# The products with the first scan batch's states, four projection steps later, in a decoder trunk on one core

## The chip, the core and the metric

The kernel runs on one core of a Trainium2 chip. The metric is the device time of one execution in microseconds (us). Engines are called by the names that the profile gives them: PE (TensorE, matrix products; its weight loads are PEld), DVE (VectorE), ACT (ScalarE), POOL (GpSimd), SP (SyncE, which here issues DMAs).

## The reference, cut to what matters

The program is a two-layer decoder trunk over 512 positions of width 1024. The change lies in layer 0, where one input projection feeds two mixers side by side: HGRN2 (a gated linear recurrence) and S5 (a complex diagonal state space model). What matters here of the S5 mixer and of the projections:

```python
proj = einsum('bld,df->blf', x, ev_w_in)          # 512 x 1024 times 1024 x 2560
q_a, f_a, i_a, g_a, u_b = split_cols(proj, [512, 512, 512, 512, 512])
# S5: 32 groups of 16 channels, 64 complex states each
drive = einsum('blgn,gpn->blgp', ug, bbar)         # real and imaginary part
h     = associative_scan(h[t] = abar * h[t-1] + drive[t])
y     = einsum('blgp,gnp->blgn', h_re, c_re) - einsum('blgp,gnp->blgn', h_im, c_im)
y     = gelu(y + d_skip * u);  z = y @ w_glu;  y_b = z[:, :512] * sigmoid(z[:, 512:])
```

HGRN2 needs q, f and g of the projection: silu(q), a log, a cumulative sum and an exp of f, silu(g). After the mixers come the output projection, a layer norm and a mixture of 16 experts; layer 1 has attention in place of the mixers.

## The kernel before, in words

Every float32 product is done as three products of halves (`hilo`, L194 to L196: ACT writes a rounded high part with a CAST, L195, and DVE subtracts it to get the low part, L196; `mm3`, L198 to L202, adds high*high, high*low and low*high in one accumulator). A weight chunk of 128 x 1024 (twice 128 rows of the contraction) is split this way three chunks ahead of its use (`split_upto`). All of this lives in a pool of 13 units `u`: raw weights, split weights and other large tiles take a unit when one is free, and the writer of a new tile waits for the last reader of the old one.

The projections of q, f and g are the main sequence of this stage: each has four chunks, and for each chunk four *steps* of six products (two rows of the contraction times three), each into one of four accumulators `acc`. In the fourth chunk each step ends with ACT's evacuation of the accumulator: Silu for q (L502), Sigmoid for f (L503), Silu for g (L505). This makes 48 steps. Between them `weave` (L57) puts pieces of a side sequence, a Python generator: a number yielded by the side says how many steps of the main sequence pass before the next piece is issued. All engines work through their instructions in the order in which they are issued, so `weave` sets the order on each of them.

The side is `s5_batches` (L916): four batches q of four pairs of groups. Within a batch:

- the *head* (L924 to L948): transposes of the input matrices VT (L928) and of the inputs U (L934), copied out of PSUM by ACT (V, L930; ut, L936), products for the inner matrix MM (L943) and their copies (L948); POOL prepares the next batch's tables
- after `YB[0]` = 1 step: the drives (L961), rotated by DVE with six operations (L964 to L969)
- after `YB[1]` = 2 steps: two scans and two products (L971 to L975)
- after `YB[2]` = 2 steps: the states H[0] (L977) and H[1] (L980)
- after `YB[3]` = 5 steps: the *products with the states* (L985, L987): for each of four r one product of ut with MM and two with H[0] and H[1], then DVE adds the result to Y (L989); the next batch's head follows at once.

The four batches take 10 steps each. Behind the last comes `glu_prep` (L993): the Gelu of Y on ACT (L998), then for four column blocks the transposes (L1005), a cast (L195) and a subtraction (L196) each. When the main sequence is at its end, what is left of the side is issued without steps in between, and then the GLU's products begin, whose first block ends with a product that needs the low part of the last weight chunk.

A second piece rides along in the g projection: `hgrn_f` (L539) gives one piece per step from step 33 on: four DVE operations on F (L544), Ln on ACT (L548), four scans on DVE (L551), Exp on ACT (L555, L556) and eight DVE products (L560, L561).

Of the kernel before, what the change touches and what calls it, by code (L numbers as in the profile page):

```python
# [35 lines left out]
YB = 1, 2, 2, 5, 0  # L36
# [16 lines left out]
def blk(i, n=128):  # L53
    return slice(i * n, (i + 1) * n)
# [23 lines left out]
def run_all(gen):  # L78
    for _ in gen:
        pass  # L80
# [82 lines left out]
class Trunk:  # L163
# [752 lines left out]
    def s5_batches(self, U, tabs):  # L916
        nc, s5, I = self.nc, self.s5, self.I
        Vv = nc.vector
        big = lambda nm: s5.tile([128, 4, 128], F32, name=nm)
        Y = U.rearrange("c r j g n -> c r j (g n)")  # L920
        f2 = lambda a: a.rearrange("p r c -> p (r c)")
        for q in range(4):
            ps, EP = slice(4 * q, 4 * q + 4), self.EPs[q % 2]
            Vm = []  # L924
            for i in range(2):
                tp = self.tp()
                for r in range(4):
                    nc.tensor.transpose(tp[:, blk(r)], self.VT[i][:, r].rearrange("p j g n -> p (j g n)"), self.idf)  # L928
                v = big(f"V{i}")
                nc.scalar.copy(v, tp.rearrange("p (r f) -> p r f", r=4))  # L930
                Vm.append(v)
            tp = self.tp()
            for r in range(4):
                nc.tensor.transpose(tp[:, blk(r)], U[:, 4 * q + r].rearrange("c j g n -> c (j g n)"), self.idf)  # L934
            ut = big("ut")
            nc.scalar.copy(ut, tp.rearrange("p (r f) -> p r f", r=4))  # L936
            nc.gpsimd.tensor_mul(Y[:, ps], Y[:, ps],
                                 self.dp[:, ps].rearrange("c r g n -> c r (g n)").unsqueeze(2).to_broadcast([128, 4, 4, 32]))
            nc.gpsimd.tensor_copy(self.R4[:, :, 1:128], self.r4[:, ps].unsqueeze(2).to_broadcast([128, 4, 127]))
            tm = self.tp()  # L940
            for r in range(4):
                for i in range(2):
                    nc.tensor.matmul(tm[0:32, blk(r)], self.BB[i][:, 4 * q + r].rearrange("p g n -> p (g n)"),  # L943
                                     EP[i][:, r, 0:4].rearrange("p k g n -> p (k g n)"),
                                     start=i == 0, stop=i == 1)
            tmv = tm.rearrange("p (r k f) -> p r k f", r=4, k=4)
            for j in range(4):
                nc.scalar.copy(self.MM[blk(j, 32), :, j:4, :], tmv[0:32, :, 0:4 - j, :])  # L948
            if q < 3:
                self.s5_inputs(q + 1)  # L950
                self.s5_outputs(q + 1)

            run_all(tabs)
            Tc, Ts = self.Tc[:, ps], self.Ts[:, ps]
            yield YB[0]

            dps = []
            for i in range(2):
                d = self.sd()
                for r in range(4):  # L960
                    nc.tensor.matmul(d[:, blk(r)], Vm[i][:, r, :], ut[:, r, :], start=True, stop=True)  # L961
                dps.append(d.rearrange("p (r c) -> p r c", r=4))
            g1, g2, h1, h2 = big("g1"), big("g2"), big("h1"), big("h2")
            Vv.tensor_mul(g1, dps[0], Tc)  # L964
            Vv.tensor_mul(h1, dps[1], Ts)
            Vv.tensor_mul(g2, dps[1], Tc)
            Vv.tensor_mul(h2, dps[0], Ts)
            Vv.tensor_add(g1, g1, h1)
            Vv.tensor_sub(g2, g2, h2)  # L969
            yield YB[1]  # L970
            Vv.tensor_tensor_scan(f2(h1), f2(self.R4), f2(g1), 0.0, op0=MUL, op1=ADD)  # L971
            Vv.tensor_tensor_scan(f2(h2), f2(self.R4), f2(g2), 0.0, op0=MUL, op1=ADD)
            a, b = slice(0, 127), slice(1, 128)
            Vv.tensor_mul(g1[:, :, a], h1[:, :, a], Tc[:, :, a])
            Vv.tensor_mul(g2[:, :, a], h2[:, :, a], Ts[:, :, a])  # L975
            yield YB[2]
            Vv.tensor_sub(self.H[0][:, :, b], g1[:, :, a], g2[:, :, a])  # L977
            Vv.tensor_mul(g1[:, :, a], h1[:, :, a], Ts[:, :, a])
            Vv.tensor_mul(g2[:, :, a], h2[:, :, a], Tc[:, :, a])
            Vv.tensor_add(self.H[1][:, :, b], g1[:, :, a], g2[:, :, a])  # L980
            yield YB[3]
            yp = self.sd()
            for r in range(4):
                o = yp[:, blk(r)]
                nc.tensor.matmul(o, ut[:, r, :], self.MM[:, r].rearrange("p l f -> p (l f)"), start=True, stop=False)  # L985
                for i in range(2):
                    nc.tensor.matmul(o, self.H[i][:, r, :], EP[i][:, r, 1:5].rearrange("p k g n -> p (k g n)"),  # L987
                                     start=False, stop=i == 1)
            Vv.tensor_add(Y[:, ps], Y[:, ps], yp.rearrange("c (r l f) -> c r l f", r=4, l=4))  # L989
            yield YB[4] if q < 3 else 3  # L990
        self.Y = Y
# [968 lines left out]
```

## Time and profile before

| | us |
|---|---|
| median of 3 runs | 991.99 (991.78 to 992.62) |
| the profiled execution's own time | 995.26 |
| its span, first to last instruction | 993.6 |
| PE busy | 859.7 (87%) |
| DVE busy | 789.4 (79%) |
| ACT busy | 571.9 (58%) |
| POOL busy | 292.1 (29%) |
| TensorE's mean granted clock | 0.945 of full |

The stage of the change lies between about 65 and 186 us of the span. A time in a timeline is that from the span's start. Products on PE overlap, so that a duration is longer than the distance from one start to the next, and the distance is what a product costs. A bracket at a row's end tells how long the engine was idle before it and which instruction ended that.

### The profile page before, as it was taken

The numbers are of one execution on the slowest core, as the hardware profiler recorded it, in microseconds if no ns is written. First come the engines' busy times: TensorE is split into PE (matmuls) and PEld (weight loads), VectorE is DVE, ScalarE is ACT, GpSimd is POOL, SyncE is SP. The second block draws the span as 40 slices with busy tenths as digits, with TensorE's granted clock in tenths as the row PEclk, the third lists the DMA queues.
The fourth block names the chain that finished last, engine by engine and source line by source line (L and its number), as shares of the span: only waits on it lengthen the run. The fifth ranks groups of instructions, "written<-read, shape, count | busy, mean of one in ns | idle before, by whom it ended". The sixth has DMA issues, their size and how long they took to land. (4 is left out here: it accounts for less than half of the span.)

```text
span 993.6 us, 13230 instructions
## 1 busy us (share of the span) xinstructions
PE 859.7 (87%) x4428; PEld 714.5 (72%) x4428; DVE 789.4 (79%) x1547; ACT 571.9 (58%) x936; POOL 292.1 (29%) x333
## 2 busy tenths in 40 slices
PE   6996999998975899999883899989994789999964
PEld 5895887787873688878662787878883668888742
DVE  7998668667679799989577757889778879999657
ACT  3331445635114889988673446666612589999741
POOL 6397981100102132221230002355611232322210
PEclk9998999999996999999897999999997799999977
DMA  8321112101946799999875350230093869999842
GB/s 274 138 87 43 43 43 94 45 1 46 361 191 231 293 296 361 393 359 309 294 246 180 129 127 1 97 74 2 1 344 148 344 222 322 374 369 362 273 126 84
DMA packets 52731, 192.02 MB, mean 193 GB/s; under 512 B 13355, under 2 KB 15415, under 8 KB 38192
## 3 DMA queue, kind: packets, MB, share of 16 engines
q1 hardware_dynamic: 37344, 156.47, 43.1%
q0 software_dynamic: 13296, 24.14, 9.3%
q10 hardware_dynamic: 2016, 10.49, 2.6%
q8 instruction: 38, 0.62, 0.3%
q14 instruction: 37, 0.30, 0.1%
HBM read 183.20 MB, written 31.46 MB: 216 GB/s over the span
## 5 line engine op out<-in xcount | busy, mean ns | idle before, releaser
L200 PE MATMUL acc<-u 128*128 128x512 f32 (+1 forms) x712 | 297.3, 418 | 7.3 <-ACT u L195 7.3
L202 PE MATMUL acc<-u 128*128 128x512 f32 (+1 forms) x712 | 282.8, 397 | 5.8 <-DVE u L196 5.6
L201 PE MATMUL acc<-u 128*128 128x512 f32 (+1 forms) x712 | 282.4, 397 | 3.4 <-POOL u L196 1.9
L196 DVE TENSOR_TENSOR u<-u 128x1024 fp32r<-128x1024 f32 x142 | 172.4, 1242 | 27.5 <-ACT u L195 26.5
L196 DVE TENSOR_TENSOR u<-rx,u 128x1024 fp32r<-128x1024 f32 x128 | 152.4, 1221 | 31.5 <-ACT u L195 30.3
L195 ACT CAST u<-u 128x1024 fp32r<-128x1024 f32 x150 | 152.9, 1050 | 42.5 <-PE acc L202 36.7
L202 PEld LDWEIGHTS acc<-u 128*128 128x128 f32 x712 | 142.0, 199 | 37.2 <-DVE u L196 9.3
L200 PEld LDWEIGHTS acc<-u 128*128 128x128 f32 x712 | 143.8, 202 | 31.2 <-ACT u L195 9.9
L201 PEld LDWEIGHTS acc<-u 128*128 128x128 f32 x712 | 142.7, 200 | 25.9 <-DVE u L196 3.4
L195 ACT CAST u<-rx 128x1024 fp32r<-128x1024 f32 x128 | 129.4, 1048 | 5.4 <-issue 3.0
L1615 POOL DMA_INDIRECT yd<-row,r x36 | 57.0, 1583 | 228.8 <-ACT row L1628 185.6
L195 ACT CAST u<-tp 128x512 fp32r<-128x512 f32 x102 | 60.1, 608 | 77.7 <-PE tp L209 62.7
L196 DVE TENSOR_TENSOR u<-tp,u 128x512 fp32r<-128x512 f32 x102 | 67.7, 700 | 12.1 <-ACT u L195 11.6
L1582 POOL DMA_INDIRECT xg<-x1d,r x41 | 46.1, 1124 | 75.6 <-PE tp L209 65.5
L209 PE MATMUL tp<-idf,xg 128*128 128x128 f32 x312 | 49.9, 302 | 17.7 <-DMA xg<-x1d,r 9.8
L209 PEld LDWEIGHTS tp<-idf,xg 128*128 128x128 f32 x312 | 47.4, 209 | 22.6 <-issue 10.1
L200 PE MATMUL acc<-u,ht 128*128 128x512 f32 x148 | 58.9, 398 | 4.0 <-ACT ht L195 4.0
L1408 POOL TENSOR_SCALAR P<-P,st 128x256 f32<-128x256 f32 (+3 forms) x32 | 35.1, 1097 | 88.6 <-DVE st L1384 55.7
L202 PE MATMUL acc<-u,ht 128*128 128x512 f32 x148 | 58.1, 392 | 0.0
L201 PE MATMUL acc<-u,ht 128*128 128x512 f32 x148 | 58.0, 392 | 0.0
L1628 ACT ACTIVATE row<-acc,r 128x512 f32<-128x512 f32 x72 | 47.1, 687 | 9.5 <-PE acc L202 9.5
L1126 ACT COPY u<-tp 128x512 f32<-128x512 f32 x16 | 9.4, 588 | 66.4 <-PE tp L1125 56.3
(428 smaller groups left out, 1453.3 us busy)
## 6 DMA issues: line engine op xcount, KB each, us to landing
rx<-in_moe_w_gate_up_dram SPq DMA_DIRECT2D x48, 1024.0 KB
u<-in_moe_w_gate_up_dram SPq DMA_DIRECT2D x24, 1024.0 KB
u<-in_moe_w_down_dram SPq DMA_DIRECT2D x19, 1024.0 KB
rx<-in_moe_w_down_dram SPq DMA_DIRECT2D x16, 1024.0 KB
u<-in_ev_w_in_dram SPq DMA_DIRECT2D x10, 1024.0 KB
u<-in_ev_w_out_dram SPq DMA_DIRECT2D x4, 1024.0 KB
x1d<-row POOLq DMA_DIRECT2D x8, 512.0 KB
yd<-row ACTq DMA_DIRECT2D x8, 512.0 KB
```

Of the source, the lines that this page charges most:

```text
L195: self.nc.scalar.copy(hi, src)
L196: (self.nc.gpsimd if pool else self.nc.vector).tensor_sub(lo, src, hi)
L200: nc.tensor.matmul(ps, ah, bh, start=start, stop=False)
L201: nc.tensor.matmul(ps, ah, bl, start=False, stop=False)
L202: nc.tensor.matmul(ps, al, bh, start=False, stop=stop)
L209: self.nc.tensor.transpose(tp[:, blk(j)], src[:, s], self.idf)
L1126: nc.scalar.copy(xt1[tt // 2][:, tt % 2, 4 * h:4 * h + 4], tp.rearrange("p (j t) -> p j t", j=4))
L1408: nc.gpsimd.tensor_scalar(P[:, 1, :W], P[:, 1, :W], st[:, 5, 1:2], None, op0=MUL)
L1582: nc.gpsimd.indirect_dma_start(out=xg, out_offset=None, in_=self.x1d, in_offset=bass.IndirectOffsetOnAxis(ap=self.toki[:, s:s + 1], axis=0 ...
L1615: return self.scattered(s, self.nc.gpsimd.indirect_dma_start(out=self.yd, out_offset=bass.IndirectOffsetOnAxis(ap=self.toki[:, s:s + 1], a ...
L1628: nc.scalar.activation(ys[:, blk(c, 512)], yp[c], AF.Copy, scale=self.gate[:, s:s + 1])
```

## The change

One line in `s5_batches`: for the first batch alone the side waits nine steps where it waited five, before the products with the states.

```diff
@@ -978,7 +978,7 @@
             Vv.tensor_add(self.H[1][:, :, b], g1[:, :, a], g2[:, :, a])
-            yield YB[3]
+            yield YB[3] + 4 if q == 0 else YB[3]
             yp = self.sd()
```

Counted in steps of the main sequence, the first batch's products with the states stood behind step 11 and stand behind step 15. All that follows in the side moves by four steps too: the second head from 11 to 15, the third from 21 to 25, the fourth from 31 to 35, the last products from 41 to 45. The Gelu was issued behind step 44, and three of the four transposed blocks behind steps 46, 47 and 48; now all of `glu_prep` is issued behind step 48. No instruction is added or removed. SP's and POOL's sequences of instructions are the same; on PE 24 products of the projection (steps 12 to 15) now stand ahead of the first L985.

On ACT, around the second batch's head, before (V_1164 and V_1171 are the copies of VT in the second batch, u the units, DVE_49 and the like the semaphores that are waited for; the two casts are those of chunks 0 and 1 of f):

```order
L195 CAST u<-u 128x1024 [waits DMAHW5_49,DVE_49,PE_49]
L195 CAST u<-u 128x1024 [waits DVE_49,PE_49]
L930 COPY V_1164<-tp 128x512 [waits PE_49,Activation_49]
L930 COPY V_1171<-tp 128x512 [waits PE_49,Activation_49]
L936 COPY ut<-tp 128x512 [waits PE_49,Activation_49]
```

and now, where the same copies are called V_1196 and V_1203 and the third cast is that of chunk 2 of f:

```order
L195 CAST u<-u 128x1024 [waits DMAHW5_49,DVE_49,PE_49]
L195 CAST u<-u 128x1024 [waits DVE_49,PE_49]
L195 CAST u<-u 128x1024 [waits DMAHW6_49,DVE_49]
L502 ACT_TABLE_LOAD
L502 ACTIVATE Q<-acc 128x512 [waits PE_49] x3
L930 COPY V_1196<-tp 128x512 [waits PE_49]
L930 COPY V_1203<-tp 128x512 [waits PE_49]
```

A cast, a table load and three evacuations of q moved ahead of the copies. This third cast now writes the unit that held the first half of f's raw weights. The DVE instruction that it waits for is the last reader of that unit, the L196 of chunk 1 of f, which stands on DVE right behind the first batch's L980; before, it took a unit that PE and an older L196 had released.

On ACT, around the fourth batch's head (F is the f projection, V_1538 and V_1578 the same copy before and now):

```order
-L195 CAST u<-u 128x1024 x2
+L195 CAST u<-u 128x1024
 L503 ACT_TABLE_LOAD
-L503 ACTIVATE F<-acc 128x512 x3
-L930 COPY V_1538<-tp 128x512
-L930 COPY V_1545<-tp 128x512
+L503 ACTIVATE F<-acc 128x512 x4
+L195 CAST u<-u 128x1024
+L548 ACT_TABLE_LOAD
+L548 ACTIVATE u<-F 128x1024 x2
+L930 COPY V_1578<-tp 128x512
+L930 COPY V_1585<-tp 128x512
```

The table load and the two Ln of `hgrn_f`, which stood behind this head, now stand ahead of its copies. They wait for the first two and for all four of DVE's L544; on DVE these stand behind the third batch's L980 and one L196, where they stood behind the fourth batch's L969 and one L196.

On DVE, from the fourth batch's rotation to its first scan, the L544 went, and L551 (scans of `hgrn_f`) came into their place, one ahead of L964 and two ahead of L971. On ACT, in front of the GLU (G is the g projection; the last four casts are those of the transposed blocks):

```order
+L195 CAST u<-u 128x1024
+L505 ACT_TABLE_LOAD
+L505 ACTIVATE G<-acc 128x512 x4
 L998 ACT_TABLE_LOAD
 L998 ACTIVATE u<-U 128x16x2x16 x4
-L195 CAST u<-u 128x1024
-L505 ACT_TABLE_LOAD
-L505 ACTIVATE G<-acc 128x512 x2
-L195 CAST u<-tp 128x4x128
```

The Gelu moved behind all four evacuations of g, of which it stood in front.

## Rows read from the trace of the kernel before

**Rows 1.** The page's first part: busy us, share of the span, instructions.

```profile
PE 859.7 (87%) x4428; PEld 714.5 (72%) x4428; DVE 789.4 (79%) x1547; ACT 571.9 (58%) x936; POOL 292.1 (29%) x333
```

**Rows 2.** PE's timeline, first products with states: start, us, line, operation, idle before.

```profile
83.78 0.39 PE L202 MATMUL acc<-u 128*128 128x512 f32 x1
84.01 0.38 PE L985 MATMUL sd<-MM,ut 128*128 128x128 f32 x2
90.59 0.79 PE L987 MATMUL sd<-EP,H 128*128 128x128 f32 x2 [6.19 <-DVE H L977]
93.24 0.80 PE L987 MATMUL sd<-EP,H 128*128 128x128 f32 x2 [1.86 <-DVE H L980]
...
97.00 1.04 PE L928 MATMUL tp<-idf,VT 128*128 128x128 f32 x8
98.33 0.66 PE L934 MATMUL tp<-idf,U 128*128 128x128 f32 x4 [0.29 <-ACT V L930]
```

**Rows 3.** DVE's timeline, the first batch's last states and what follows them.

```profile
92.42 0.77 DVE L980 TENSOR_TENSOR H<-g,g 128x508 f32<-128x508 f32 x1
93.10 1.21 DVE L196 TENSOR_TENSOR u<-u 128x1024 fp32r<-128x1024 f32 x1
```

**Rows 4.** ACT's timeline: a cast of a chunk; two evacuations of f.

```profile
102.70 1.05 ACT L195 CAST u<-u 128x1024 fp32r<-128x1024 f32 x1
...
137.59 1.09 ACT L503 ACTIVATE F<-acc 128x512 f32<-128x512 f32 x2
```

**Rows 5.** Busy us by stretch: PE, PEld, DVE, ACT, POOL, granted clock, DMA, GB/s.

```profile
94.00:95.00 1.00, 1.00 (x7) 1.00 (x6) 0.31 (x1) 0.00 (x0) 0.00 (x0) 0.50 0.00 0
...
176.00:177.00 1.00, 1.00 (x4) 0.76 (x3) 0.74 (x1) 0.98 (x2) 1.00 (x2) 0.50 0.00 0
```

**Rows 6.** PE's timeline, second batch's products with states, fourth batch's head.

```profile
117.43 0.49 PE L987 MATMUL sd<-EP,H 128*128 128x128 f32 x2 [0.48 <-DVE H L980]
...
119.76 1.04 PE L928 MATMUL tp<-idf,VT 128*128 128x128 f32 x8
...
143.85 0.66 PE L934 MATMUL tp<-idf,U 128*128 128x128 f32 x4 [0.29 <-ACT V L930]
```

**Rows 7.** DVE's timeline, third batch's end and fourth batch.

```profile
140.05 1.26 DVE L196 TENSOR_TENSOR u<-u 128x1024 fp32r<-128x1024 f32 x1
...
153.91 1.91 DVE L544 TENSOR_SCALAR F<-F,lbo,lb 128x512 f32<-128x512 f32 x4
...
159.17 1.22 DVE L551 TENSOR_TENSOR_SCAN u<-dsk,u 128x512 f32<-128x512 f32 x1
```

**Rows 8.** ACT's timeline, fourth batch's head and the Ln.

```profile
143.21 1.07 ACT L930 COPY V<-tp 128x512 f32<-128x512 f32 x2 [3.31 <-PE tp L928]
...
154.99 1.28 ACT L548 ACT_TABLE_LOAD   x1 [5.24 <-DVE F L544]
156.28 2.01 ACT L548 ACTIVATE u<-F 128x1024 f32<-128x1024 f32 x2
```

**Rows 9.** PE's timeline, last products with states to the first GLU block.

```profile
163.06 0.49 PE L987 MATMUL sd<-EP,H 128*128 128x128 f32 x2 [0.59 <-DVE H L980]
...
172.03 0.39 PE L202 MATMUL acc<-u 128*128 128x512 f32 x1
173.78 0.33 PE L1005 MATMUL tp<-idf,u 128*128 128x128 f32 x1 [1.36 <-ACT u L998]
...
182.16 0.66 PE L1005 MATMUL tp<-idf,u 128*128 128x128 f32 x4 [0.65 <-DVE u L196]
...
186.26 0.51 PE L202 MATMUL acc<-u 128*128 128x512 f32 x1 [0.62 <-DVE u L196]
```

**Rows 10.** ACT's timeline, the Gelu and a cast of a transposed block.

```profile
173.10 2.19 ACT L998 ACTIVATE u<-U 128x512 f32<-128x512 f32 x4
...
181.54 1.08 ACT L195 CAST u<-tp 128x512 fp32r<-128x512 f32 x1
```

**Rows 11.** DVE's timeline, the subtraction of a transposed block.

```profile
182.65 1.08 DVE L196 TENSOR_TENSOR u<-tp,u 128x512 fp32r<-128x512 f32 x1 [0.55 <-ACT u L195]
```

## The prediction

> **What bounds the kernel now.** I read the page's busy shares first, then busy time by stretches of this stage, then the timelines of PE, DVE and ACT beside each other, and last the order of the changed program. PE is the engine to follow: it is busy for 87% of the span [rows 1], and in this stage nearly always, so that a stall of PE here ends up in the total. Its largest gap of the stage is the one that the change aims at. At 84.01 PE issues the first products with the states and then waits 6.19 us for H[0] and 1.86 us for H[1] [rows 2], while DVE is still working off the rotation tables. Behind the gap the granted clock is 0.50, that is 1.2 GHz in place of 2.4 [rows 5], and the products from 93.24 to 97.00 take 3.76 us [rows 2], where the same piece of the second batch, from 117.43 to 119.76, takes 2.33 us [rows 6].
>
> **The change part by part.** Nothing is added or removed; four steps go ahead of the first products, and the rest of the side comes four steps later against the projection. I go along the side's course, since PE has to issue it in order.
>
> *The first gap.* A product of the projection costs 0.23 us (83.78 to 84.01 [rows 2]). The 24 products moved ahead are 24 x 0.23 = 5.5 us of work, and they need nothing that DVE still has to do. PE comes to L985 at 84.0 + 5.5 = 89.5 and still waits for H[0] (90.59) and H[1] (93.24), since DVE's chain is the same. So 5.5 us of the 8.05 us of waiting are filled. The clock will hardly be better there, as what is left of the wait is nearly all of the time from 89.9 to 93.2; I let PE arrive at the second head at 97.0 as before.
>
> *The second head.* Here the change takes something back. ACT's copies of VT (L930), for which L934 waits, now stand behind a cast, a table load and three evacuations. The cast waits for the L196 behind L980, which ends at 93.10 + 1.21 = 94.31 [rows 3]. From there: cast 1.05 and three evacuations of 1.09 / 2 each, 1.64 [rows 4], a table load of 1.28 [rows 8], in sum 98.28, and from L930 to L934 the 0.64 us of the fourth head (143.21 [rows 8] to 143.85 [rows 6]): L934 at 98.92 in place of 98.33 [rows 2], 0.6 us late. Slow clock or not, PE is at L928 early enough for this. Left of the gain: -5.5 + 0.6 = -4.9 us. Were the cast free of its wait, the products would decide (97.0 or, at the full clock, 95.6); with one more wait in front of it all of the 5.5 could go. I take -4.9, bounds -6.9 and 0.
>
> *The second and third batch* keep their place relative to the chunks, since four steps are one chunk: one cast and one L196 fall where one fell. Cost 0, covered by the same nine steps between the drives and the products; the wait for H[1] (0.48 us [rows 6]) stays.
>
> *The fourth head.* Now `hgrn_f` begins ahead of it. The third batch's L980 ends when the L196 behind it starts, at 140.05 [rows 7]. From there: L196 1.26, two of the four L544 0.96 [rows 7], table load 1.28, two Ln 2.01 [rows 8]: L930 could start at 145.56, where it started at 143.21 [rows 8]. L934, the rest of the head and the drives wait for it: +2.4 us on PE, which has only L928 in that time. No cover: the step behind the head stands behind L934 on PE. At the least it is 1.4 (one Ln less in front, were ACT to take L930 between them, which the order excludes), at the most 3.4, if all four L544 come first.
>
> *The clock behind that stall.* PE then idles 2.4 + 0.29 = 2.7 us. In this trace the clock fell to 0.50 behind the gap of 8 us, and also behind a 1.36 us wait with a few transposes after it (173.78 [rows 9], the clock at 176 [rows 5]). So I take it to fall here too, and price it by the first case: 3.76 - 2.33 = 1.4 us. Bounds 0 and 1.7.
>
> *The fourth batch's chain.* On DVE two L551 (1.22 each with their ends overlapped, 2.3 in sum) stand ahead of the scans where four L544 stood (1.91 [rows 7]): +0.4. One more L551 stands ahead of L964; it starts when the step behind the head is done, most of it beside the drives on PE; 0.3 to 0.4 sticks out. PE already waits 0.59 us for this H[1] [rows 9], so it has no slack to give: +0.8 us. Bounds 0.4, with that L551 wholly beside the drives, and 1.5, with none of it beside them.
>
> *The end.* Before, Gelu and transposes lay among steps 44 to 48. From the last product of step 46 (172.03 + 0.23 = 172.26) to the last product of the first GLU block at 186.26 [rows 9] it took 14.0 us, with two steps of 6 x 0.23 = 1.4 us in it: 11.2 us without them. Now all stands behind step 48, counted from its end: evacuation about 0.9 with its start, table load 1.28 [rows 8], so Gelu begins at 2.2; L989 on DVE is done earlier than that. The first transpose is 0.68 us behind Gelu's start (173.10 [rows 10], 173.78 [rows 9]), the last of the first block behind the fourth Gelu, at 2.2 + 2.19 + 0.4 = 4.8. The two buffers of `tp` then set the pace: cast 1.08 [rows 10] and subtraction 1.08 [rows 11] of the first block free its buffer, a further subtraction of 1.1 the second's, so the fourth block's transposes start at 4.8 + 3.3 = 8.1. From there to the last product of the GLU block it took 186.26 - 182.16 = 4.1 us [rows 9]: 12.2 in sum, against 11.2. So +1.0 us; bounds 0 and 2.4, the upper one if the clock falls in this gap and 1.4 us of GLU products are paid at half speed.
>
> **Sum.** -4.9 + 2.4 + 1.4 + 0.8 + 1.0 = +0.7 us. The stages behind hang on PE's and DVE's work in order, so I let the shift through unchanged. Against the profiled execution's own 995.26 us (span 993.6) this is 996.0; the runs' median of 991.99 is 3.3 us lower, and the sum is in absolute us, so the forecast is 991.99 + 0.7 = 992.7.
>
> A rule that speaks against the change: three table loads now stand in front of something PE waits for. In the row, the first Ln starts at 156.28, right where the load of 154.99 ends after 1.28 us [rows 8]. The Trainium skill, "ScalarE: Activation LUTs", section "What ACT_TABLE_LOAD costs", puts about 1.38 us of draining on top of a load of about 1.28. By the row the sum stays +0.7; by that page it would be 3 x 1.38 = 4.1 us more, an estimate. The trace agrees with the load and shows no drain behind it, so I stay with the row.
>
> **The rivals.**
> 1. *Gain kept.* The third stall leaves the clock up: everything above without 1.4 is -0.7, 991.3. If also the second head's cast is not late (its wait done earlier than I place it), -6.9 + 2.4 + 0.8 + 1.0 = -2.7, 989.3. For it: PE's gap of 8.05 us is the largest of the stage, and 24 products fit into it without a wait. Against it: the cast's last reader is an instruction that DVE reaches only behind L980 [rows 3].
> 2. *The end decides: slower.* Behind step 48 PE has nothing but transposes for 8 us; if the clock is down when the GLU begins, another 1.4 us goes: +2.1, 994.1; with the upper bounds of the fourth head (+1.0) and of the chain (+0.7) as well +3.8, 995.8. It decides as soon as what is given back exceeds the 4.9 by more than 2 us. For it: a wait as short as 1.36 us brought the clock down [rows 9, 5]. Against it: in that stretch PE mostly waits for casts anyway, which don't slow down.
> 3. *Table loads cost double*, each once more its 1.28 us [rows 8]: +0.7 + 3 x 1.28 = +4.5, 996.5. Against it the row itself.
> 4. *No effect that can be measured*, because gain and give-back cancel to the us: that is the forecast itself, by its mechanism.
>
> **How the numbers follow.** What a measurement of this kernel can tell from no change is about 0.2%, 2 us: 990.0 to 994.0. Forecast (around +0.7, scatter 1.5 us either way) 0.40: within 0.33, slower 0.05, faster 0.02. Rival 1: 0.30, half of it with the clock alone (within 0.13, faster 0.02) and half with the cast too (within 0.03, faster 0.12). Rival 2: 0.27 (slower 0.22, within 0.05). Rival 3: 0.03, slower. Sum: faster 0.16, within 0.54, slower 0.30. The range goes from rival 1's lower end to rival 2's upper one: 989.3 to 995.8; the likeliest case's own is 991.2 to 994.2.
>
> **What will show it.** In the changed trace: L985 of the first batch some 5.5 us later, with about 3 us of waits where there were 8; the first L934 waiting for L930 by about 1 us more than 0.29, with L930 starting behind L502 near 98.3; the fourth L934 idle about 2.7 us behind L930, with two Ln right in front of it on ACT; a granted clock of 0.50 behind it; the wait for the fourth H[1] above 1 us; the first L1005 idle near 2.8 us. It is wrong if the second head's L934 comes later than 100 (the gain gone there), if the fourth L934 waits less than 1 us, or if the time after the GLU's start moves by more than a us against the GLU's start.

## The result, and the profile after

The changed kernel takes 1001.14 us (median of 4 runs, 998.62 to 1004.28) where the kernel before took 991.88 beside it, 9.3 us less. The recorded ratio, which is not the quotient of these two medians, is 1.0082 with a 95% interval of 1.0060 to 1.0103, which makes some 8 us; a second set of runs further below gives 7.4 us by its medians and 1.0085. So it is slower by 7 to 9 us; the forecast was 992.7 us, the range ended at 995.8. The profiled execution took 1004.28 us (span 1002.6) against 995.26 (span 993.6).

The page's first part, as in [rows 1], does not show the place: DVE and ACT are as busy as before to within 1 us. PE is busy for 8.0 us more with as many instructions, at a mean granted clock of 0.934 in place of 0.945.

```profile
PE 867.7 (87%) x4428; PEld 721.2 (72%) x4428; DVE 788.6 (79%) x1547; ACT 571.8 (57%) x936; POOL 294.0 (29%) x333
```

To find the loss I compared the same instructions of PE in both timelines, from one landmark to the next. For the kernel before, landmarks that stand in none of the groups are these: the drives of the second and of the fourth batch, the last products with states and the step behind them, and the first HGRN transposes (L598), behind which the distance hardly grows any more (columns as in [rows 2]).

```profile
102.27 1.95 PE L961 MATMUL sd<-ut,V 128*128 128x128 f32 x16
...
147.79 1.95 PE L961 MATMUL sd<-ut,V 128*128 128x128 f32 x16
...
161.86 0.38 PE L985 MATMUL sd<-MM,ut 128*128 128x128 f32 x2
...
165.31 0.49 PE L200 MATMUL acc<-u 128*128 128x512 f32 x1
...
186.61 0.60 PE L598 MATMUL tp<-idf,F 128*128 128x128 f32 x4
```

And PE's timeline of the changed kernel from the first products with states to the same transposes:

```profile
89.41 0.38 PE L985 MATMUL sd<-MM,ut 128*128 128x128 f32 x2
90.62 0.49 PE L987 MATMUL sd<-EP,H 128*128 128x128 f32 x2 [0.83 <-DVE H L977]
93.27 0.49 PE L987 MATMUL sd<-EP,H 128*128 128x128 f32 x2 [2.16 <-DVE H L980]
...
95.61 1.04 PE L928 MATMUL tp<-idf,VT 128*128 128x128 f32 x8
98.85 0.66 PE L934 MATMUL tp<-idf,U 128*128 128x128 f32 x4 [2.21 <-ACT V L930]
...
102.80 1.95 PE L961 MATMUL sd<-ut,V 128*128 128x128 f32 x16
...
143.02 1.04 PE L928 MATMUL tp<-idf,VT 128*128 128x128 f32 x8
147.11 1.11 PE L934 MATMUL tp<-idf,U 128*128 128x128 f32 x4 [3.06 <-ACT V L930]
...
153.88 1.95 PE L961 MATMUL sd<-ut,V 128*128 128x128 f32 x16
...
167.92 0.38 PE L985 MATMUL sd<-MM,ut 128*128 128x128 f32 x2
171.06 0.79 PE L987 MATMUL sd<-EP,H 128*128 128x128 f32 x2 [2.76 <-DVE H L977]
173.11 0.79 PE L987 MATMUL sd<-EP,H 128*128 128x128 f32 x2 [1.26 <-DVE H L980]
...
177.27 0.48 PE L200 MATMUL acc<-u 128*128 128x512 f32 x1
...
184.24 2.89 PE L1005 MATMUL tp<-idf,u 128*128 128x128 f32 x8 [2.63 <-ACT u L998]
188.54 2.10 PE L1005 MATMUL tp<-idf,u 128*128 128x128 f32 x8 [1.41 <-DVE u L196]
...
194.94 0.60 PE L598 MATMUL tp<-idf,F 128*128 128x128 f32 x4
```

Worked out from these rows, in us (a step is 6 x 0.227 = 1.36, four are 5.46):

| stretch | before | after | difference | predicted |
|---|---|---|---|---|
| to the second batch's drives, after with four steps more done | 102.27 | 102.80 - 5.46 = 97.34 | -4.9 | -4.9 |
| second to fourth drives: the wait for V at the fourth head | 0.29 | 3.06 | +2.8 | +2.4 |
| the same: L934 to the drives, same instructions | 3.94 | 6.77 | +2.8 | +1.4 |
| fourth drives to the last L985 | 14.07 | 14.04 | 0.0 | 0 |
| last L985 to the step behind the products | 3.45 | 9.35 | **+5.9** | **+0.8** |
| from there to L598, before with four steps less | 21.30 - 5.46 = 15.84 | 17.67 | +1.8 | +1.0 |
| sum, = 194.94 - 186.61 | | | +8.3 | +0.7 |

The front did what was expected of it. The fourth batch did not, and DVE's and ACT's timelines of the changed kernel show why. DVE first:

```profile
158.27 0.68 DVE L969 TENSOR_TENSOR g<-g,h 128x512 f32<-128x512 f32 x1
162.41 1.23 DVE L196 TENSOR_TENSOR u<-u 128x1024 fp32r<-128x1024 f32 x1 [3.46 <-ACT u L195]
163.55 2.33 DVE L551 TENSOR_TENSOR_SCAN u<-dsk,u 128x512 f32<-128x512 f32 x2
165.80 1.20 DVE L971 TENSOR_TENSOR_SCAN h<-R,g 128x512 f32<-128x512 f32 x1
...
170.34 0.66 DVE L977 TENSOR_TENSOR H<-g,g 128x508 f32<-128x508 f32 x1
...
172.37 0.69 DVE L980 TENSOR_TENSOR H<-g,g 128x508 f32<-128x508 f32 x1
```

and ACT, with the Ln of the fourth head and the cast that the L196 of 162.41 waits for:

```profile
143.28 1.28 ACT L548 ACT_TABLE_LOAD   x1 [6.03 <-DVE F L544]
144.58 2.00 ACT L548 ACTIVATE u<-F 128x1024 f32<-128x1024 f32 x2
146.49 1.05 ACT L930 COPY V<-tp 128x512 f32<-128x512 f32 x2
...
161.32 1.05 ACT L195 CAST u<-u 128x1024 fp32r<-128x1024 f32 x1 [7.82 <-PE acc L202]
```

The L196 is the low part of the GLU's first weight chunk. By the program's order its cast writes the unit in which the low part of the first half of x lay, the input that all the projections share; PE reads this half for the last time in g's second chunk, which ends with step 40, at 161.1 (167.92 less five steps). The trace agrees: the cast's wait of 7.82 us ends with a product of the projection, and in the six other profiles in which this cast waits it starts within 0.3 us of the end of step 40. So the cast comes at 161.32, the subtraction at 162.41, and behind it two L551 and the fourth batch's scans wait on DVE, although what they need was there at 158.95. In the kernel before, this L196 stands behind the fourth batch's L980. A subtraction stood ahead of the scans there too, that of the last chunk of g, but its cast had long been done (it starts at 148.71 on ACT), and it did not wait. DVE before:

```profile
152.78 1.22 DVE L196 TENSOR_TENSOR u<-u 128x1024 fp32r<-128x1024 f32 x1
...
162.92 1.22 DVE L196 TENSOR_TENSOR u<-u 128x1024 fp32r<-128x1024 f32 x1
```

The order on DVE, from the end of the fourth batch's rotation:

```
before                                  after
L969 g                                  L969 g
L196 (g's last chunk, low part)         L196 (GLU's first chunk, low part)
L544 F x4                               L551 x2
L971 scan                               L971 scan
...                                     ...
L980 H[1]                               L980 H[1]
L196 (GLU's first chunk, low part)
```

That a ready instruction does not pass a waiting one is shown by the 3.46 us in which DVE did nothing, though the Ln that the L551 read had ended at 146.58. The Trainium skill, "TensorE: Matmul & The Clock Gate", section "Architectural detail: the array is 16× 32×32, not 1× 128×128", says the same of VectorE's and ScalarE's queues in a remark: strictly first in, first out.

The clock fell at all three places in this execution. The granted clock by stretch, columns as in [rows 5]:

```profile
146.00:154.00 8.00, 6.89 (x28) 5.29 (x29) 0.00 (x0) 3.79 (x8) 1.82 (x2) 0.57 0.00 0
170.00:177.00 7.00, 4.68 (x20) 4.39 (x21) 6.93 (x11) 4.93 (x5) 0.22 (x1) 0.52 0.17 66
184.00:194.00 10.00, 8.21 (x25) 5.90 (x26) 5.26 (x5) 6.65 (x9) 0.94 (x5) 0.50 0.07 27
```

0.50 is 1.2 GHz in place of 2.4. Behind the front's remaining waits it stayed full in this execution, unlike in [rows 5]: L985 to L928 took 6.2 us.

### The profile page after: what moved, and what is told of

Read it like the earlier page. It is cut to its first block, busy times and chain, and to the rows that moved or that the text cites. A ratio compares the mean times of both kernels' runs of the same rounds, so it can differ in the third digit from the quotient of the medians.

```text
span 1002.6 us, 13219 instructions
## 1 busy us (share of the span) xinstructions
PE 867.7 (87%) x4428; PEld 721.2 (72%) x4428; DVE 788.6 (79%) x1547; ACT 571.8 (57%) x936; POOL 294.0 (29%) x333
## 5 line engine op out<-in xcount | busy, mean ns | idle before, releaser
L196 DVE TENSOR_TENSOR u<-u 128x1024 fp32r<-128x1024 f32 x142 | 171.7, 1237 | 29.8 <-ACT u L195 28.9
L196 DVE TENSOR_TENSOR u<-rx,u 128x1024 fp32r<-128x1024 f32 x128 | 152.3, 1220 | 29.3 <-ACT u L195 28.2
L196 DVE TENSOR_TENSOR u<-tp,u 128x512 fp32r<-128x512 f32 x102 | 67.7, 699 | 20.0 <-ACT u L195 19.6
L209 PE MATMUL tp<-idf,xg 128*128 128x128 f32 x312 | 51.1, 308 | 14.7 <-DMA xg<-x1d,r 9.8
```

The lines of the kernel that those rows point to most:

```text
L196: (self.nc.gpsimd if pool else self.nc.vector).tensor_sub(lo, src, hi)
L209: self.nc.tensor.transpose(tp[:, blk(j)], src[:, s], self.idf)
```

## The experiments

Ratios are to the kernel before, timed on the same chip beside each run; the median there was 992.9 to 993.7 us. "The repairs" are the edits of the first two experiments.

### The split of the GLU's first chunk one chunk later

```diff
-    def tok(self, c0, evac, sel):
+    def tok(self, c0, evac, sel, ahead=None):
-            hi, lo = self.chunk(c0 + c)
+            hi, lo = self.chunk(c0 + c, ahead and ahead.get(c))
...
-                for _ in self.tok(c["g"], ..., lambda j: blk(j)):
+                for _ in self.tok(c["g"], ..., lambda j: blk(j), {1: 2}):
```

> The changed kernel with one edit: the split of the GLU block's chunk 0 is issued one chunk of the g projection later, so that its low part's cast and subtraction stand behind the fourth batch's scans and products, no more ahead of them. Theory A (the cast waits for a unit that only step 40 of the projections frees, the subtraction waits for the cast, and the fourth batch's scans stand behind the subtraction): the chain from the fourth head's first vector operation to its state H falls from 9.3 us to about 4.5 us, TensorE's wait ahead of the fourth batch's products with states from 2.8 us to under 1 us, and the time from about 1001 to about 996.5 us (some +4.5 us over the kernel before). Theory B (VectorE is simply full there: head, two decay scans, batch scans): the subtraction moves but the scans start no earlier than 1 us before now; time about 1000 us. Theory C (what was lost is the lower clock, which falls behind any gap in this stage): the wait goes, but the clock is still 0.50 for some 6 us there; time about 998.5 us.

Measured: 992.5 us, ratio 0.9998 (0.9980 to 1.0016). Nearly the whole loss is gone. DVE's timeline: the scans follow L969 with two L551 between and no wait, and the L196, now two, stands behind L980:

```profile
156.07 0.69 DVE L969 TENSOR_TENSOR g<-g,h 128x512 f32<-128x512 f32 x1
156.67 2.33 DVE L551 TENSOR_TENSOR_SCAN u<-dsk,u 128x512 f32<-128x512 f32 x2
158.92 1.20 DVE L971 TENSOR_TENSOR_SCAN h<-R,g 128x512 f32<-128x512 f32 x1
...
165.50 0.69 DVE L980 TENSOR_TENSOR H<-g,g 128x508 f32<-128x508 f32 x1
166.10 2.35 DVE L196 TENSOR_TENSOR u<-u 128x1024 fp32r<-128x1024 f32 x2
```

On PE the last L985 starts at 165.72 and the step behind the products at 168.50: 2.8 us for 9.35. The gain, 8.6 us by the medians and 8.3 by the ratios, is more than the 4.5 that Theory A gave it. 6.6 us of it (9.35 less 2.78) are in this stretch, 4.0 of them waits; Theory A had left out the products at half clock. The fourth head's wait is 3.06 us as before, and from L934 (146.12) to the drives (151.68) it is 5.56 us where it was 6.77; where the rest of the gain lies the runs don't show. B and C are refuted: the scans start 2.2 us behind the end of L969 in place of 6.9, and the granted clock is 1.00 from 165 to 169.

### The Ln behind the fourth head

```diff
-                for _ in self.tok(c["g"], ...):
-                    next(decay, None)
+                for i, _ in enumerate(self.tok(c["g"], ...)):
+                    for _ in range((1, 0, 0, 2, 2)[i] if i < 5 else 1):
+                        next(decay, None)
```

> The changed kernel with one edit: the pieces of the HGRN decay are handed out at other steps of the g projection (1, 0, 0, 2, 2, then one each), so that the table load and the two Ln come on ScalarE behind the fourth batch's copies of V, no more ahead of them. The split of the GLU block's chunk 0 stays where it is. Theory A (the load and the Ln ahead of the copies cost the fourth head 2.8 us of waiting and a stretch of lower clock behind it another 2.8 us): TensorE's wait for the second copy of V falls from 3.06 us to about 0.3 us, the clock stays full through the fourth head, and the time goes from about 1001 to about 995.5 us; the wait for the cast at the fourth batch's scans stays, as does the end. Theory B (the fourth chain's cast wait absorbs whatever the head loses, since it hangs on step 40 only): step 40 itself comes earlier by what the head gains, so this is a loss of the gain only if decay scans pushed later stand ahead of the batch's scans; then about 998 to 1000 us. Theory C (the lower clock would come at another gap): only the 2.8 us of waiting are gained, about 998.3 us.

Measured: 997.18 us, ratio 1.0031 (1.0013 to 1.0049), less than the changed kernel by 4.0 us (medians) or 5.1 us (ratios). Theory A's signs hold, its time of 995.5 does not quite. PE's timeline (the edit adds a line above, so that L934 is L935 here, and L987 is L988):

```profile
144.77 0.66 PE L935 MATMUL tp<-idf,U 128*128 128x128 f32 x4 [0.29 <-ACT V L931]
...
166.81 0.79 PE L988 MATMUL sd<-EP,H 128*128 128x128 f32 x2 [3.64 <-DVE H L978]
```

The head's wait is 0.29 again and its clock full, from drives to drives it is 45.5 us as before. The fourth batch's wait stays and is even longer. The edit itself does that: with the pieces handed out later, three L551 (3.45 us) stand ahead of the scans in place of two (2.33 us).

### Both repairs

> The changed kernel with both edits: the decay's Ln behind the fourth head and the split of the GLU block's chunk 0 one chunk later. Theory A (both losses are of the order of work on ScalarE and VectorE around the fourth batch, and independent): the front's gain of 4.9 us shows, less about 2 us at the end of the stage and 1 us of the chain: about 989 to 990.5 us, faster than the kernel before by 1 to 3 us. Theory B (the fourth batch four steps nearer to the stage's end always costs what the front gains): within 1 us of the kernel before or slower, 991.5 to 994 us. Theory C (the lower clock comes whatever the waits are): 994 to 996 us.

Measured: 990.91 us, ratio 0.9973 (0.9956 to 0.9990): Theory A's 1 to 3 us, faster than the kernel before, at the upper end of its time. By the ratios the two repairs gain 8.3 and 5.1 us alone and 10.8 together. Part of the difference is the third L551 ahead of the scans, which the second repair brings: the fourth batch has 1.00 us of waiting again, where the first repair alone left none. What is left against the front's gain is the end, where PE waits for the Gelu with nothing to do:

```profile
163.25 0.49 PE L988 MATMUL sd<-EP,H 128*128 128x128 f32 x2 [1.00 <-DVE H L981]
...
172.74 0.33 PE L1006 MATMUL tp<-idf,u 128*128 128x128 f32 x1 [2.86 <-ACT u L999]
```

### The four steps behind the second batch

```diff
-            yield YB[3] + 4 if q == 0 else YB[3]
+            yield YB[3] + 4 if q == 1 else YB[3]
```

> The kernel before with the four steps put behind the second batch in place of the first: the first batch's products with states stand behind step 11 as before, the third and fourth batches' heads and products four steps later, as in the changed kernel. Theory A (the front gains 4.9 us by the filled gap ahead of the first batch's products and the losses are all in the fourth batch and the end): the first gap comes back and every loss stays: about 1006 us, 14 us over the kernel before. Theory B (part of the loss comes from the first batch's longer hold of its units and of ScalarE's order in the steps 11 to 15): losses are smaller, about 1003 us. Theory C (the losses are the lower clock that a fuller front brings later): without the fuller front the lower clock of the fourth batch is not there, about 997 to 1000 us.

Measured: 1005.28 us, ratio 1.0120 (1.0093 to 1.0146). Theory A, some 2 us below its number: the first gap is back, and the losses are all there though the first batch is that of the kernel before. Behind the same wait of 3.06 us the clock cost less than in the first profile of the changed kernel: L934 to the drives took 5.57 us for 6.77.

```profile
90.16 0.80 PE L987 MATMUL sd<-EP,H 128*128 128x128 f32 x2 [6.26 <-DVE H L977]
...
151.88 0.66 PE L934 MATMUL tp<-idf,U 128*128 128x128 f32 x4 [3.06 <-ACT V L930]
...
157.45 1.95 PE L961 MATMUL sd<-ut,V 128*128 128x128 f32 x16
...
174.65 0.49 PE L987 MATMUL sd<-EP,H 128*128 128x128 f32 x2 [2.75 <-DVE H L977]
```

### The changed kernel once more

No edit.

> The changed kernel once more, unaltered, to see how much its own time scatters and whether the places of the loss repeat. Theory A (the order of work sets the losses): again about 1.007 to 1.009 times the kernel before, with 3.06 us of waiting at the fourth head, two waits of 2.8 and 1.3 us ahead of the fourth batch's products with states, and the lower clock in both places. Theory B (the lower clock came by chance in the one profile): the clock is full at one of the two places, and the time is 3 us or more below 1001 us.

Measured: 1001.11 us (996.83 to 1004.70, 6 runs), ratio 1.0085 (1.0059 to 1.0111). The waits repeat (3.06, then 2.76 and 1.57 us), so the order sets them. The clock does not repeat everywhere: in this profile (span 997.6) it was full behind the 3.06 us wait at the fourth head, and L934 to the drives took 3.94 us in place of 6.77. So the clock cost 2.8 us there in the first profile and nothing in this one, for the same instructions behind the same wait. At the front it was the other way round: L985 to L928 took 7.4 us here, with the lower clock, and 6.2 in the first profile. Of theory B the first half holds too: the lower clock is there in one execution and not in the other.

```profile
146.00:154.00 8.00, 7.62 (x51) 6.66 (x52) 3.41 (x5) 3.05 (x7) 1.81 (x2) 1.00 0.00 0
170.00:177.00 7.00, 7.00 (x30) 6.43 (x30) 7.00 (x11) 2.48 (x3) 2.06 (x4) 0.60 0.09 27
```

### The later split in the kernel before

The edit of the first experiment, made in the kernel before.

> The kernel before with the one edit that issues the split of the GLU block's chunk 0 one chunk of the g projection later. Theory A (the edit only repairs a wait that the change made): there the low part stood behind the fourth batch's scans already, so within 1 us of the kernel before. Theory B (the later split is a gain by itself, and the experiment on the changed kernel showed that gain on top of a repair): 3 us or more faster than the kernel before.

Measured: 993.54 us, ratio 1.0007 (0.9993 to 1.0020). The edit is no gain by itself; on the changed kernel it repaired what the change had put there.

### One step and two steps

```diff
-            yield YB[3] + 4 if q == 0 else YB[3]
+            yield YB[3] + 1 if q == 0 else YB[3]      # the other kernel: + 2
```

> The change at a quarter of its size: one step in place of four. The Ln stand behind the fourth head; on VectorE the low part of the GLU block's chunk 0, which waits for its cast till step 40 is done, stands between the fourth batch's scans and its H. Theory A (a place in the order decides, and not the size of the shift): front -1.4, fourth batch +3 to +4, end +0.5: about 994 to 995 us, as slow as two steps or slower, though only a quarter of the shift. Theory B (the loss grows with the shift): +0.5 to +2 us less than with two steps, so 992.5 us, within 0.1% of the kernel before.

> The change at half its size: two steps in place of four. The Ln then stand behind the fourth head on ScalarE (as in the kernel before), while on VectorE the low part of the GLU block's chunk 0 stands between the fourth batch's scans and its H. Theory A (the fourth batch loses as soon as that subtraction stands ahead of H, whatever the size of the shift): front -2.7, fourth batch some +6, end +1: about 996 us, 4 us over the kernel before, with a wait of 3 to 4 us ahead of the fourth batch's products with states and none of 3 us at the fourth head. Theory B (the loss grows in step with the shift): half of +9, about 996 to 997 us too, but with half the wait at either place. Theory C (only the head's stall and the clock behind it decide): 989 to 991 us.

Measured: one step 997.90 us, ratio 1.0051 (1.0031 to 1.0071); two steps 995.14 us, 1.0019 (1.0005 to 1.0032). So the loss does not grow in step with the shift: one step costs no less than two. By the ratios it costs more (5.1 and 1.9 us); in the two profiles this stage, from the first drives to the HGRN transposes, takes 120.3 and 119.7 us, 116.7 before. Counted against the kernel before by the ratios, Theory A's numbers were 2 to 3 us too low for one step (+2 to +3 expected, +5.1 measured) and 2 us too high for two (+4, +1.9). With two steps the Ln stand behind the head (wait 0.29) and the L196 between the fourth batch's scans and H, where it waits 1.66 us for its cast; PE then waits 0.93 and 1.55 us. With one step the waits there are 1.18 and 1.55 us, but not for the reason that Theory A gave: the L196 between scans and H starts at 162.64 without a wait, and the batch is late because a subtraction that waited for its cast and the four L544 stand ahead of its rotation (L964 at 154.48, the drives at 150.00). And a subtraction has come between scans and H in the *second* batch as well, which I had not foreseen. DVE and, behind it, PE:

```profile
114.52 1.77 DVE L196 TENSOR_TENSOR u<-u 128x1024 fp32r<-128x1024 f32 x1
116.21 0.87 DVE L977 TENSOR_TENSOR H<-g,g 128x508 f32<-128x508 f32 x1
```

```profile
119.64 0.49 PE L987 MATMUL sd<-EP,H 128*128 128x128 f32 x2 [2.01 <-DVE H L980]
```

It waits for nothing there; its own duration is enough, since that chain has no slack (0.48 us of waiting before [rows 6], 2.01 now). The one that stood ahead of the scans before now stands ahead of that batch's rotation, where it takes about as long with the wait for its cast.

### Both repairs and a shorter end

The Gelu follows the last products at once, and the decay's last DVE products stand behind Y's last addition:

```diff
-                    for _ in range((1, 0, 0, 2, 2)[i] if i < 5 else 1):
+                    for _ in range((1, 0, 0, 2, 2, 1, 1, 1, 1, 0, 0, 0, 0, 4, 0, 0)[i]):
...                                            # in hgrn_f: all Exp first, then L560, L561
             yield
+        for i in range(2):
             for h in (2 * i, 2 * i + 1):
...
-            yield YB[4] if q < 3 else 3
+            yield YB[4]
```

> The changed kernel with both repairs, and with the end shortened: the Gelu follows step 45 at once (no more step 48), its table is loaded between two evacuations of G, and the decay's last products of Q and F stand behind the last batch's sum on VectorE, no more ahead of it. Theory A (the end lost what covers the Gelu: four steps before, none after): TensorE's first transposes of the GLU block wait for nothing or under 1 us in place of 2.86 us, and the time is 2 to 3 us below the version with both repairs, about 0.9945 to 0.9955 times the kernel before. Theory B (the casts and subtractions behind the transposes set the end, and the second table load delays these): no more than 0.5 us, about 0.997. Theory C (the lower clock comes at another gap): between the two.

Measured: 988.51 us, ratio 0.9949 (0.9929 to 0.9968), as Theory A said, and the best version: 5 us faster than the kernel before. ACT's timeline (two lines added above, L998 is L1000), with the Gelu's load between two evacuations of G:

```profile
165.00 0.60 ACT L505 ACTIVATE G<-acc 128x512 f32<-128x512 f32 x1
165.62 1.28 ACT L1000 ACT_TABLE_LOAD   x1
167.25 2.19 ACT L1000 ACTIVATE u<-U 128x512 f32<-128x512 f32 x4 [0.34 <-DVE U L991]
169.46 1.28 ACT L505 ACT_TABLE_LOAD   x1
```

The first transposes stand at 168.37 on PE without a wait. From the step behind the products to the HGRN transposes it takes 14.7 us (165.51 to 180.19), against 17.5 with the repairs alone (165.51 to 183.04); the medians differ by 2.4 us.

### The best version without the shift, twice

First with the shift simply taken back:

```diff
-            yield YB[3] + 4 if q == 0 else YB[3]
+            yield YB[3]
```

> The best version so far (both repairs and the shortened end) with the change itself taken back: the first batch's products stand behind step 11 again. Theory A (the four steps in the first gap are what the best version gains, 4.9 us in its front): 3 to 5 us over the best version, so 0.998 to 1.0 times the kernel before, with a wait of about 6.2 us ahead of the first batch's second products. Theory B (the best version is faster for its repairs and its end alone, and the shift adds nothing): as fast as the best version, 0.995.

Measured: 1004.53 us, ratio 1.0101 (1.0076 to 1.0126): neither theory, and the run doesn't tell what the shift is worth. The decay's schedule had been fitted to the shifted order. The Gelu, now behind step 41, stands on ACT behind the Exp, whose scans had been put off, and PE waits for it longer than ever:

```profile
173.37 2.03 PE L1007 MATMUL tp<-idf,u 128*128 128x128 f32 x4 [6.25 <-ACT u L1000]
```

So a second run kept the order behind the second batch and moved the four steps there:

```diff
-            yield YB[3] + 4 if q == 0 else YB[3]
+            yield YB[3] + 4 if q == 1 else YB[3]
```

> The best version so far (both repairs and the shortened end) with the four steps put behind the second batch in place of the first: everything from the third batch on stands in the same order as in the best version, only the gap ahead of the first batch's products is back. Theory A (the filled gap is worth about 4.9 us, and the version without the shift was slow because its Gelu stood behind the exponentials, which stood behind the delayed decay scans): 4 to 5.5 us over the best version, 0.9995 to 1.0005 times the kernel before. Theory B (the shift brings nothing of its own): 0.995.

Measured: 992.11 us, ratio 0.9993 (0.9977 to 1.0010), 4.4 us over the best version by the ratios (0.9993 and 0.9949). Theory A: this is what the filled first gap is worth once nothing behind it is paid for.

## Why the prediction was wrong

- **The first gap and the second head**: right. L985 at 89.41 (predicted 89.5), L934 at 98.85 (98.92), together -4.9 us as predicted. The two pairs with the steps behind the second batch give somewhat less (4.4 us in the best version; 1.0120 against 1.0082 and 1.0085, some 3.6 us, in the changed kernel); there the shift also fills the second batch's own wait of 0.48 us. That the clock would stay low there failed in the first profile and came true in the second, without a cost: from L985 to L934 it took 9.4 and 9.5 us, since ACT's copies set the second head's time at either level.
- **The second and third batch**: right, no change.
- **The fourth head**: right in mechanism and nearly in size, 2.8 us for 2.4. The load's row repeats: Ln starts at 144.58, where the load of 143.28 ends (143.28 + 1.28 = 144.56). The drain of 1.38 us of the Trainium skill, "ScalarE: Activation LUTs", "What ACT_TABLE_LOAD costs", is not seen here either; rival 3 is out.
- **The clock behind that stall**: one number was taken for what differs from one execution to the next. I took 1.4 us from another stretch, with bounds of 0 and 1.7. Behind the same 3.06 us wait the runs show 2.8 us and none in the changed kernel's two profiles, and 1.6 us with the later split and with the steps behind the second batch (5.56 and 5.57 us for 3.94). So the first profile's 2.8 is outside the bounds, and nothing that I read says beforehand which of the three it will be.
- **The fourth batch's chain**: this step failed, +5.9 us where the prediction put +0.8, with 1.5 as its upper bound. It weighed two L551 against four L544 ahead of the scans and left out the L196 between them. One stands there in either order, so its 1.2 us cancel; but four steps later is one chunk later, and so it is now that of the next chunk. For the second and third batch I said that one cast and one L196 fall where one fell, and there it cost nothing; at the fourth batch I did not ask what the next one waits for. This was the error: a subtraction waits for a cast, the cast for a unit, the unit for step 40, and this date stays with the projection while the scans had come four steps nearer to it. Of the 5.9 us, 3.4 are waits (2.76 + 1.26 for 0.59); the rest is mostly the products behind them at half clock (173.11 to 177.27 for 163.06 to 165.31, +1.9).
- **The end**: +1.8 us where +1.0 stood, within its bounds. The best version shows that this loss can be avoided.
- **Rival 2** had the sign, and the place only in part: the losses behind exceed the gain, but most of the excess is at the fourth batch and not at the end. No rival had the wait that decided. Two of the signs of being wrong that the prediction named, a second head's L934 later than 100 and a fourth L934 that waits less than 1 us, did not come (98.85 and 3.06 us); its sign for the failed step, a wait for the fourth H[1] above 1 us, came true (1.26 us), and the 2.76 us for H[0] in front of it had none.

What stays open: why the granted clock falls behind the same wait in one execution and not in another, and where the part of the first repair's gain lies that the fourth batch does not show.

## What to carry to other kernels

When a piece of work is moved in an order that several engines share, list for each engine what now stands between two links of its chains, and for each such instruction when its *inputs and its buffer* are free, not only how long it runs. Dates that belong to the main sequence (a buffer released by its 40th step) don't move with the side. Then move the obstacle and not the gain back: here two repairs of the order turned +8 us into -3, and an earlier Gelu made it -5.

## What was not expected of the hardware

The changed kernel's runs scatter more than those of the kernel before in the first comparison: 998.62 to 1004.28 us against 991.27 to 992.62. Much of this difference goes away with more runs: all ten of the changed kernel lie between 996.83 and 1004.70, the 29 of the kernel before beside the first experiments between 990.68 and 996.81. In the first four runs of the changed kernel the mean granted clock goes with the time: 0.934 at 1004.28, 0.937 at 1002.0, 0.938 at 1000.29 and 0.944 at 998.62.

A wait of about 3 us did not have the same effect everywhere: behind 3.06 us at the fourth head the clock fell in one profile of the changed kernel and stayed full in the other; behind 0.83 and 2.16 us at the front it stayed full, as in the best version (6.2 us from the first L985 to the next L928 in both); in the profile with the two repairs alone, behind 0.78 and 2.16 us of waiting, the same piece took 7.7 us, with products at half clock, and in the second profile of the changed kernel, behind 1.53 and 1.55 us, 7.4 us.
